# State-space stage of a hybrid backbone: pair decays by a minimum of two differences of running sums, initial state entered token-major

## Chip, core, metric

One core of a Trainium2 chip. The time is the device time of one launch in microseconds, as the median of three runs: 1575.97 us for the kernel before (1575.73 to 1576.37).

## What is computed

Two layers of a diffusion backbone run over 256 tokens: 128 context tokens (group 0) and 128 latent tokens (group 1), model width 1024. A layer is a half-step SwiGLU, a mixer with three branches (a bidirectional state-space scan, differential attention, pooling), and another half-step SwiGLU. The change touches only the scan. The scan has 16 heads of width 64, a state of 64, four groups of B and C, and one chunk of 128 tokens, so that for one direction it is

```python
a = (dt * a_coef)                                  # (heads, 128 tokens), negative
a_cum = jnp.cumsum(a, axis=-1)
seg = a_cum[..., :, None] - a_cum[..., None, :]
decay_in = jnp.exp(jnp.where(causal, seg, -jnp.inf))
scores = einsum('bclhn,bcshn->bchls', ch, bh) * decay_in
y_diag = einsum('bchls,bcshp->bclhp', scores, xdt)
decay_from_start = jnp.exp(a_cum)
y_off = einsum('bclhn,bchpn,bchl->bclhp', ch, h_prev, decay_from_start)
```

The backward direction is the same on the reversed tokens; both are added. The initial state h_prev is zero for the context tokens and is an input for the latent ones, so y_off exists for group 1 alone.

## The kernel before

**The main stream.** Everything that multiplies by a weight runs as a list of tiles of 128x1024 weights in a fixed order (`plan`, L155). A weight tile is loaded (`raw`, L567 to 576), copied by ScalarE to a rounded high part (`wh`, `emit_hi` L578) and its remainder is formed by VectorE (`wl`, `emit_lo` L588). Every product is three matmuls, high by high, high by low, low by high (`mm3`, L629), into three rotating PSUM tiles `pm`. The high parts are made five tiles ahead of use and the low parts four (`HI_AHEAD`, `LO_AHEAD`), in `end` (L610).

**Side work.** All else, the scan too, is written as Python generators that are advanced between pairs of weight blocks of the main stream (`advance`, L534). A generator yields the engine that its next step begins on and what the step waits for; `Pace` (L335) keeps an estimated clock of each engine and of each buffer, and `due` (L528) lets a step on TensorE be issued when its inputs are estimated to be ready, and a step on another engine when that engine is estimated to be at most 4 us ahead of TensorE. Two generators of the list `gens` run at a time (`CONC`). So the order on each engine is fixed at build time; the waits are semaphores that the framework places. PSUM for side work is two tiles `s1` of one bank and one tile `s2` of two banks (L482 to 486). The names `s1` and `s2` stand in the trace as `s`. SBUF work tiles of 128x1024 come from one pool `big` of 27 (L50, L452). All loads are issued by SyncE in one queue.

**The mixer** (L1049) runs in this order: dt, the gate of the pooling branch, x/B/C; pooling input and Q in two halves; the pooling branch; K; V; then it waits, in the order of issue, for the scan to be issued (`settle` on "y"); z; the gates and projections of the scan branch, and of the attention branch after `flush` (all side work issued); the output. The scan's generators start as soon as x/B/C are there and run beside pooling input, Q, the pooling projection and K. The attention's scores start when K is there.

**The scan before.** `ssd_prep` (L1400) makes dt and a token-major, splits a into a rounded part `ah` and a rest `al`, and forms with two small matmuls the decay to the end of the chunk (`dd`). `ssd_core` (L1472) goes through four iterations: two halves of the heads (`hf`, eight heads each) by two groups (`g`). In each iteration and for each direction `rhs` (L1507) writes `rh` and `rl`, 128 tokens x 8 heads x 128: a triangle of ones times the value of a (one VectorE instruction for `ah`, eight ScalarE ones for `al`). A product with a constant triangle `cstr` sums over tokens and gives the pair differences: 2 directions x 2 banks x 2 parts = 8 matmuls of 512 columns into `s2`, one direction masked to zero where the other holds. One ScalarE exp of 128x1024 makes the decays `ex`; VectorE multiplies them by the masked scores `cbm`, once per direction (`E`); 16 matmuls with xdt give y in `py`. For g = 1, 8 more matmuls with the ones halves of `cstr` (L1580) put the running sums across partitions, exp and a product with C give `CE`, and 8 fp32 matmuls with the block-diagonal initial state `h04` (L1615) are added into `py` ahead of the others. The state is loaded once for each half (L1484). A plain fp32 matmul shows as two records in the trace; a rounded one (fp32r) and a transpose as one.

All compute instructions go through one helper, so the profile puts them on L397; loads are on L568.

Of the kernel before, what the change touches and what calls it, by code (L numbers as in the profile page):

```python
# [10 lines left out]
F32 = mybir.dt.float32  # L11
# [38 lines left out]
BIG_BUFS = 27  # L50
# [47 lines left out]
for _n, _w in (("ident", 128), ("ones", 128), ("sel", 2), ("uf", 128), ("ub", 128), ("p0", 128), ("p1", 128), ("p2", 128),  # L98
               ("p3", 128), ("cos", 128), ("sin", 128), ("perm", 128), ("mf", 128), ("mb", 128), ("oh0", 128),
               ("oh1", 128)):  # L100
    CST[_n] = (_o, _o + _w)
    _o += _w
CST_W = _o
CST_R0 = CST["mf"][0]
# [3 lines left out]
def constants():  # L108
# [12 lines left out]
    put("mf", k > m)  # L121
    put("mb", k < m)
    put("oh0", np.broadcast_to(m < 64, (P, P)))
    put("oh1", np.broadcast_to(m >= 64, (P, P)))
# [189 lines left out]
def pack_small(I):  # L314
# [8 lines left out]
    bd = np.zeros((DEPTH, P, 2, 8, P), np.float32)  # L323
    for T in range(8):
        for half in range(2):
            h = ho[2 * T + half]
            bd[:, 64 * half:64 * half + 64, :, T, 64 * half:64 * half + 64] = st[:, :, h].transpose(0, 3, 1, 2)
    return xT, cT, ck, cv, np.ascontiguousarray(bd.reshape(DEPTH, P, 2, 2, 4, P).transpose(0, 3, 1, 2, 4, 5)).reshape(DEPTH, 2, P, 1024)
# [99 lines left out]
def backbone(ctx: ExitStack, tc: tile.TileContext, seq, wst, wada, wa0, wrow, xT_d, cT_d, cB_d, ck_d, cv_d, h0_d, prm_d, cst_d,  # L428
# [59 lines left out]
    cst = cp.tile([P, CST_R0], F32, name="cst")  # L488
# [5 lines left out]
    cstr = cp.tile([P, 4, P], F32R, name="cstr")  # L494
# [485 lines left out]
    def setup_consts():  # L980
        load(cst[:, CST_E:], cst_d[:, CST_E:CST_R0])
        ld = tmp("t512", [P, 512])
        load(ld, cst_d[:, CST_R0:CST_W])
        yield "dve", ld
        V.tensor_copy(cstr.rearrange("p a b -> p (a b)"), ld)
# [414 lines left out]
    def ssd_prep(l, sd):  # L1400
# [44 lines left out]
        ah, al = t64("dtah", F32R), t64("dtal", F32)  # L1445
        yield "dve", a
        V.tensor_copy(ah, a)
        yield "dve", ah
# [7 lines left out]
        V.tensor_tensor(out=dd, in0=pd, in1=a[:, 0], op=ALU.subtract)  # L1456
        drop("s1", pd)
        yield "act", dd
# [11 lines left out]
        sd.update(dt=dt, ah=ah, al=al, dd=dd, Bn=Bn)  # L1470

    def ssd_core(l, sd, yv):  # L1472
# [8 lines left out]
        def prep(it):  # L1481
            hf, g = its[it]
            if g == 0:
                h0 = big()  # L1484
                load(h0, h0_d[l, hf])
                half_[hf] = [h0.rearrange("p (d t q) -> p d t q", d=2, t=4), None]
# [20 lines left out]
        def rhs(it, d):  # L1507
            hf, g = its[it]
            rh = v3(big(F32R), 8)
            rl = v3(big(F32R), 8)  # L1510
            uu = C("uf" if d == 0 else "ub")
            yield "dve",
            if d < RH_ACT:
                for h in range(8):
                    c = d * 16 + hf * 8 + h
                    S.activation(out=rh[:, h], in_=uu, func=AF.Copy, scale=sd["ah"].bitcast(F32)[:, g, c:c + 1])
            else:
                V.tensor_tensor(out=rh, in0=uu.unsqueeze(1).to_broadcast([P, 8, P]),
                                in1=sd["ah"][:, g, hd(hf)[d]].unsqueeze(2).to_broadcast([P, 8, P]), op=ALU.mult)
            yield "act",  # L1520
            for h in range(8):
                c = d * 16 + hf * 8 + h
                S.activation(out=rl[:, h], in_=uu, func=AF.Copy, scale=sd["al"][:, g, c:c + 1])
            state[it, d] = (rh, rl)

        yield from prep(0)
        yield from rhs(0, 0)
        for it, (hf, g) in enumerate(its):
            xdt, xw = state.pop(it)
            yield from rhs(it, 1)  # L1530
            if g == 0:
# [14 lines left out]
                half_[hf][1] = cbm  # L1546
# [16 lines left out]
            h04, cbm = half_[hf]  # L1563
            CE = []
            ps = None
            for d in range(2):
                rh, rl = state.pop((it, d))
                if d == 0:
                    yield "pe", rh, rl, "s2"
                    ps = ps2()  # L1570
                else:
                    yield "pe", rh, rl
                for q in range(2):
                    T_.matmul(ps[:, q, :], lhsT=cstr[:, d], rhs=rh[:, 4 * q:4 * q + 4], start=(d == 0), stop=False)
                    T_.matmul(ps[:, q, :], lhsT=cstr[:, d], rhs=rl[:, 4 * q:4 * q + 4], start=False, stop=(d == 1))
                if g == 1:
                    yield "pe", "s1"
                    pr = ps1(512)
                    rh4 = rh.rearrange("p (j h) t -> p j h t", h=2)
                    rl4 = rl.rearrange("p (j h) t -> p j h t", h=2)  # L1580
# [3 lines left out]
                    ce = tmp("ce", [P, 4, P])  # L1584
                    yield "act", pr
                    S.activation(out=ce.rearrange("p a b -> p (a b)"), in_=pr, func=AF.Exp)
                    drop("s1", pr)
                    CE.append(ce)
                rh = rl = None
            yield "act", ps  # L1590
            ex = big()
            S.activation(out=ex, in_=ps.rearrange("p a b -> p (a b)"), func=AF.Exp)
            drop("s2", ps)
            if it < 3:
                yield from prep(it + 1)
            for ce in CE:
                yield "dve", ce
                V.tensor_tensor(out=ce, in0=ce, in1=BC[:, 1, hf, P:].unsqueeze(1).to_broadcast([P, 4, P]), op=ALU.mult)
# [8 lines left out]
            if it < 3:  # L1607
                yield from rhs(it + 1, 0)
            yield "pe", E[0], E[1], "s1"
            py = ps1(512)  # L1610
            for j in range(4):
                sl = slice(j * P, (j + 1) * P)
                if g == 1:
                    for d in range(2):
                        T_.matmul(py[:, sl], lhsT=h04[:, d, j, :], rhs=CE[d][:, j], start=(d == 0), stop=False)  # L1615
                for d in range(2):
                    for half in range(2):
                        T_.matmul(py[64 * half:64 * half + 64, sl],
                                  lhsT=xdt[:, d, j * P + half * 64:j * P + half * 64 + 64],
                                  rhs=E[d][:, 2 * j + half], start=(g == 0 and d == 0), stop=(d == 1))  # L1620
# [191 lines left out]
```

## Time and profile before

| | |
|---|---|
| median of 3 runs | 1575.97 us |
| span of the profiled execution | 1579.0 us |
| TensorE matmul busy | 1547.9 us |
| VectorE busy | 1313.5 us |
| ScalarE busy | 877.7 us |
| GpSimd busy | 58.7 us |
| HBM read, written | 343.36 MB, 4.19 MB |

The profile is one execution. Its span, first to last instruction, is what the rows below add up to; it is 3.0 us above the median of the runs, and no time outside the span is shown. A matmul's own duration contains its way through the array, so matmuls overlap: the cost of one in a stream is read from the distance of starts, not from its duration. In the timeline, equal neighbours are merged into one row with a count.

### The profile page before, as it was taken

Reading aid. Unit: us, or ns where it says so; the run is one execution under the profiler, and the core shown is the slowest. Engines: PE = TensorE matmul, PEld = TensorE weight load, DVE = VectorE, ACT = ScalarE, POOL = GpSimd, SP = SyncE. Lnnn points to the kernel's source line nnn. Section 1 sums busy time; section 2 is a strip of 40 time slices with the busy share of each in tenths; the row PEclk is TensorE's granted clock in tenths of the full one; section 3 lists DMA queues with packets and bytes.
Section 4 is the critical chain, followed back from the end, with each engine's and each line's share of the span. In section 5 each row is a group of like instructions: output and inputs, shape, how many; then the busy total and the mean of one; then the engine's idle time right before and its main releaser. Section 6 shows DMA issues by size and latency. Waiting matters only on the chain.

```text
span 1579.0 us, 31076 instructions
## 1 busy us (share of the span) xinstructions
PE 1547.9 (98%) x12154; PEld 1449.6 (92%) x12154; DVE 1313.5 (83%) x2391; ACT 877.7 (56%) x1640; POOL 58.7 (4%) x65
## 2 busy tenths in 40 slices
PE   6999999999999999999999999999999999999997
PEld 4998889999979999899899998998998999999986
DVE  4777798988598997899989999898768889989754
ACT  3564447676467446644547544576746754665442
POOL 0000002000001100100001000100000010010000
PEclk9999999999999999999999999999999999999998
DMA  9698764553674666687765877555447457557652
GB/s 365 210 336 291 280 247 168 189 174 114 219 241 155 214 241 221 216 300 286 261 221 195 301 268 268 181 187 177 138 146 278 166 206 258 177 200 282 218 181 81
DMA packets 99171, 349.59 MB, mean 221 GB/s; under 512 B 10960, under 2 KB 14672, under 8 KB 98896
## 3 DMA queue, kind: packets, MB, share of 16 engines
q1 hardware_dynamic: 99024, 347.60, 62.4%
q8 instruction: 96, 1.57, 0.4%
q14 instruction: 51, 0.42, 0.1%
HBM read 343.36 MB, written 4.19 MB: 220 GB/s over the span
## 4 chain that ended last, share of the span: by engine, by line
PE 76%; issue 12%; DVE 7%; DMA 3%; ACT 1%; POOL 1%; DVEq 0%; SPq 0%; POOLq 0%; ACTq 0%
PE pm L397 67%; PE s L397 7%; DVE wl L397 2%; DVE big L397 2%; PE pa L397 2%; DMA big<-wada 2%; DVE t1k L397 1%; POOL osr L397 1%; DVE wide L397 0%; DMA t<-prm 0%; DMA x<-xT 0%; ACT big L397 0%; DVE sqa L397 0%; ACT L397 0%; ACT t1k L397 0%
## 5 line engine op out<-in xcount | busy, mean ns | idle before, releaser
L397 PE MATMUL pm<-big,wh 128*128 128x256 f32 (+2 forms) x6568 | 1288.8, 293 | 2.5 <-DVE wide L397 1.6
L397 PEld LDWEIGHTS pm<-big,wh 128*128 128x128 f32 x6568 | 1028.5, 189 | 46.3 <-issue 16.4
L397 PE MATMUL pm<-big,wl 128*128 128x256 f32 (+1 forms) x3592 | 1004.1, 281 | 0.0
L397 PEld LDWEIGHTS pm<-big,wl 128*128 128x128 f32 x3592 | 676.7, 188 | 2.4
L397 DVE TENSOR_TENSOR wl<-raw,wh 128x1024 fp32r<-128x1024 f32 x481 | 586.4, 1224 | 25.3 <-ACT wh L397 25.0
L397 ACT CAST wh<-raw 128x1024 fp32r<-128x1024 f32 x481 | 501.3, 1047 | 135.2 <-PE pm L397 105.4
L397 DVE SCALAR_TENSOR_TENSOR big<-big,big 128x1024 f32<-128x1024 f32 x198 | 241.4, 1219 | 9.7 <-DMA big<-wrow 8.6
L397 ACT CAST big<-t1k 128x256 fp32r<-128x256 f32 x88 | 35.8, 407 | 151.8 <-DVE t1k L397 151.8
L397 ACT ACTIVATE big<-x,amod 128x128 fp32r<-128x128 f32 x96 | 33.4, 396 | 100.9 <-DVE x L397 81.0
L397 PE MATMUL pm<-wh,big 128*128 128x512 f32 x256 | 88.5, 409 | 0.0
L397 DVE TENSOR_TENSOR wide<-pm,rb 128x258 f32<-128x258 f32 (+1 forms) x108 | 45.1, 421 | 39.2 <-PE pm L397 33.5
L397 DVE SCALAR_TENSOR_TENSOR x<-pm,mods,x 128x128 f32<-128x128 f32 x152 | 43.6, 343 | 37.1 <-PE pm L397 36.9
L397 ACT COPY big<-pm 128x256 f32<-128x256 f32 (+2 forms) x88 | 30.7, 372 | 59.2 <-PE pm L397 58.5
L397 PEld LDWEIGHTS pm<-wh,big 128*128 128x128 f32 x256 | 48.1, 188 | 13.2 <-issue 2.1
L397 DVE TENSOR_TENSOR big<-t1k,big 128x256 fp32r<-128x256 f32 x128 | 55.5, 438 | 1.6 <-ACT big L397 0.9
L397 ACT ACTIVATE t1k<-wide 128x128 f32<-128x128 f32 (+1 forms) x96 | 33.4, 395 | 38.3 <-DVE wide L397 38.2
L397 PE MATMUL s<-big,big 128*64 128x128 f32 (+4 forms) x528 | 51.4, 295 | 0.0
L397 PE MATMUL pm<-wl,big 128*128 128x512 f32 x128 | 50.4, 394 | 0.0
L397 ACT ACTIVATE t1k<-pm 128x256 f32<-128x256 f32 x58 | 22.3, 385 | 49.4 <-PE pm L397 49.4
L397 PEld LDWEIGHTS s<-big,big 128*64 128x64 f32 (+2 forms) x528 | 40.8, 163 | 5.9 <-issue 2.3
L397 DVE TENSOR_TENSOR big<-big,big 128x256 f32<-128x256 f32 (+1 forms) x64 | 39.9, 623 | 3.7 <-ACT big L397 2.3
L397 DVE SCALAR_TENSOR_TENSOR big<-big,cw,big 128x252 f32<-128x252 f32 (+1 forms) x96 | 39.2, 473 | 2.5 <-ACT big L397 2.5
(142 smaller groups left out, 1001.7 us busy)
## 6 DMA issues: line engine op xcount, KB each, us to landing
raw<-wst SPq DMA_DIRECT2D x486, 512.0 KB, 3.8
big<-wrow SPq DMA_DIRECT2D x96, 512.0 KB, 5.2
big<-wada SPq DMA_DIRECT2D x32, 512.0 KB, 5.8
big<-wa SPq DMA_DIRECT2D x16, 512.0 KB, 10.2
big<-cB SPq DMA_DIRECT2D x12, 512.0 KB, 7.0
big<-h SPq DMA_DIRECT2D x4, 512.0 KB, 4.7
x<-xT SPq DMA_DIRECT2D x1, 1024.0 KB, 6.0
ns<-t SPq DMA_DIRECT2D x8, 128.0 KB, 3.5
```

The source lines that it names most:

```text
L397: r = fn(*a, **k)
```

## The change

The pair decay of forward and backward is exp of the smaller of two differences: with running sums from both sides, the difference that belongs to the direction in force is negative and the other positive. So no triangles are written. `ssd_prep` forms both running sums by two matmuls of 64 columns, copies them token-major into `c4` (four copies, for four rows per head), transposes that (2 transposes), and keeps it rounded with its rest in rows (`ch`); 64 of these rows go into a stationary operand `ltc`, each half masked for a direction. `ssd_core` writes one moving operand for an iteration, `zc` (64 of its rows by VectorE from `ch`; the other 64 are constants), and forms the two differences in 2 matmuls for each half of 512 columns. ScalarE copies one to SBUF, VectorE takes the minimum with the other, ScalarE takes the exp: two rounds of this an iteration. The initial state is stored dense for both halves of heads in one tile, loaded once; for g = 1 two matmuls with 64 rows each give C times state token-major, VectorE multiplies by the decays `ec` and adds the directions to `ys`, and four transposing matmuls put `ys` into `py`. `big` has 25 tiles. The constants mf, mb, oh0, oh1 go, bm (16 columns) and ind (2) come.

```diff
-BIG_BUFS = 27
+BIG_BUFS = 25
...
+    put("bm", np.where(k < 64, 1.0, -1.0) * (k % 16 == m[:, :16]))
+    put("ind", k // 16 % 2 == m[:, :2])
...
-    cstr = cp.tile([P, 4, P], F32R, name="cstr")
+    ltc = cp.tile([P, 2, 2, P], F32R, name="ltc")
+    zc = [cp.tile([P, 8, P], F32R, name=f"zc{hf}") for hf in range(2)]
...
 def ssd_prep
-        ah, al = t64("dtah", F32R), t64("dtal", F32)
-        V.tensor_copy(ah, a)
-        V.tensor_tensor(out=al, in0=a, in1=ah, op=ALU.subtract)
-        pd = ps1(32)
-        T_.matmul(pd[:, 0:16], lhsT=C("ub"), rhs=a[:, 0, 0:16], start=True, stop=True)
-        T_.matmul(pd[:, 16:32], lhsT=C("uf"), rhs=a[:, 0, 16:32], start=True, stop=True)
+        pd = ps1(128)
+        for i, u in enumerate(("uf", "ub")):
+            T_.matmul(pd[:, 64 * i:64 * i + 64], lhsT=C(u), rhs=a.rearrange("p g c -> p (g c)"), start=True, stop=True)
...
+        for d in range(2):
+            V.tensor_copy(c4[:, :, :, d, :], p4[:, d, :, d, :].unsqueeze(2).to_broadcast([P, 2, 4, 16]))
+            V.tensor_tensor(out=dd[:, 16 * d:16 * d + 16], ..., op=ALU.subtract)
...
+            T_.transpose(pc[:, g * P:(g + 1) * P], c4[:, g].rearrange("p c d h -> p (c d h)"), C("ident"))
...
+        S.copy(ch.rearrange("p a b -> p (a b)"), pc)
...
+            S.activation(out=ec[:, :, :, d, :], in_=c4[:, 1, 0, d].rearrange(...), func=AF.Exp)
+        for q in (32, 96):
+            V.tensor_tensor(out=ch[q:q + 32], in0=v3(pc, 2)[q:q + 32], in1=ch[q:q + 32].bitcast(F32), op=ALU.subtract)
...
+            V.tensor_scalar(out=ltc[64:P, d], in0=ch[64:P].bitcast(F32), scalar1=C("ind")[64:P, d:d + 1], ...)
...
 def ssd_core
-            if g == 0:
+            if it == 0:
                 h0 = big()
-                load(h0, h0_d[l, hf])
+                load(h0, h0_d[l])
...
-        def rhs(it, d):
+        def lines(it):
+            V.tensor_tensor(out=zc[hf][0:64], in0=sd["ch"][0:64, g]..., in1=C("bm")[0:64, hf * 8:hf * 8 + 8]..., op=ALU.mult)
...
-                for q in range(2):
-                    T_.matmul(ps[:, q, :], lhsT=cstr[:, d], rhs=rh[:, 4 * q:4 * q + 4], start=(d == 0), stop=False)
-                    T_.matmul(ps[:, q, :], lhsT=cstr[:, d], rhs=rl[:, 4 * q:4 * q + 4], start=False, stop=(d == 1))
-                if g == 1:
-                    for half in range(2):
-                        T_.matmul(pr, lhsT=cstr[:, 2 + half], rhs=rh4[:, :, half, :], start=(half == 0), stop=False)
-                        T_.matmul(pr, lhsT=cstr[:, 2 + half], rhs=rl4[:, :, half, :], start=False, stop=(half == 1))
-                    S.activation(out=ce.rearrange("p a b -> p (a b)"), in_=pr, func=AF.Exp)
-            S.activation(out=ex, in_=ps.rearrange("p a b -> p (a b)"), func=AF.Exp)
+            for q in range(2):
+                yield "pe", ltc, zc[hf], "s2"
+                ps = ps2()
+                for d in range(2):
+                    T_.matmul(ps[:, d, :], lhsT=ltc[:, d, g], rhs=zc[hf][:, 4 * q:4 * q + 4], start=True, stop=True)
+                S.copy(eq, ps[:, 0, :])
+                V.tensor_tensor(out=eq, in0=ps[:, 1, :], in1=eq, op=ALU.min)
+                drop("s2", ps)
+                S.activation(out=eq, in_=eq, func=AF.Exp)
+            if it < 3:
+                yield from lines(it + 1)
+            if g == 1:
+                yield "pe", half_["h0"], "s2"
+                for half in range(2):
+                    pr = slice(64 * half, 64 * half + 64)
+                    T_.matmul(ps[:, half, :], lhsT=BC[pr, 1, hf, P:], rhs=half_["h0"][pr, hf], start=True, stop=True)
+                V.tensor_tensor(out=v3(yo, 16), in0=ps..., in1=sd["ec"]..., op=ALU.mult)
+                V.tensor_tensor(out=ys.rearrange("p j h q -> p h j q"), in0=y5[:, :, 0], in1=y5[:, :, 1], op=ALU.add)
...
-                V.tensor_tensor(out=ce, in0=ce, in1=BC[:, 1, hf, P:].unsqueeze(1).to_broadcast([P, 4, P]), op=ALU.mult)
...
+            if g == 1:
+                for j in range(4):
+                    T_.matmul(py[:, j * P:(j + 1) * P], lhsT=ys[:, j].rearrange("p h q -> p (h q)"), rhs=C("ident"),
+                              is_transpose=True, start=(j == 0), stop=False, skip_group_check=True)
...
-                        T_.matmul(py[:, sl], lhsT=h04[:, d, j, :], rhs=CE[d][:, j], start=(d == 0), stop=False)
```

## Rows read from the trace of the kernel before

**Rows 1.** Page, parts 1 and 4: engines' busy time; the chain by engine.

```profile
PE 1547.9 (98%) x12154; PEld 1449.6 (92%) x12154; DVE 1313.5 (83%) x2391; ACT 877.7 (56%) x1640; POOL 58.7 (4%) x65
...
PE 76%; issue 12%; DVE 7%; DMA 3%; ACT 1%; POOL 1%; DVEq 0%; SPq 0%; POOLq 0%; ACTq 0%
```

**Rows 2.** Stretches of layer 0: us, busy of each engine (instructions), clock, DMA.

```profile
core 0: us, PE busy (x) PEld busy (x) DVE busy (x) ACT busy (x) POOL busy (x), PEclk, DMA share, GB/s
...
330.00:343.00 13.00, 13.00 (x103) 10.79 (x102) 11.03 (x19) 11.08 (x27) 0.00 (x0) 1.00 0.34 125
343.00:402.00 59.00, 59.00 (x506) 52.78 (x505) 44.72 (x64) 35.76 (x81) 0.00 (x0) 1.00 0.38 126
402.00:436.00 34.00, 34.00 (x291) 34.00 (x290) 20.78 (x28) 18.03 (x29) 0.00 (x0) 1.00 0.73 259
436.00:500.00 64.00, 63.99 (x432) 54.74 (x431) 58.81 (x116) 44.87 (x126) 0.00 (x0) 1.00 0.59 197
...
525.00:597.00 72.00, 72.00 (x614) 72.00 (x614) 67.00 (x115) 32.31 (x51) 1.44 (x2) 1.00 0.64 227
597.00:680.00 83.00, 79.34 (x666) 76.41 (x665) 69.84 (x146) 53.15 (x97) 6.63 (x9) 1.00 0.65 228
```

**Rows 3.** Timeline, TensorE, scan of layer 0: start, length, instruction, count.

```profile
342.96 2.03 PE L397 MATMUL s<-big,cstr 128*128 128x512 f32 x8
344.83 0.39 PE L397 MATMUL pm<-wh,big 128*128 128x512 f32 x1
345.06 0.39 PE L397 MATMUL pm<-wl,big 128*128 128x512 f32 x1
...
345.52 0.60 PE L397 MATMUL s<-cst,big 128*128 128x128 f32 x4
345.87 0.48 PE L397 MATMUL pm<-wh,big 128*128 128x512 f32 x1
346.19 0.39 PE L397 MATMUL pm<-wl,big 128*128 128x512 f32 x1
...
350.24 1.97 PE L397 MATMUL s<-big,big 128*64 128x128 f32 x32
352.14 0.71 PE L397 MATMUL s<-cst,big 128*128 128x128 f32 x4
352.61 1.17 PE L397 MATMUL s<-big,cstr 128*128 128x512 f32 x4
...
368.11 0.61 PE L397 MATMUL s<-ce,big 128*128 128x128 f32 x4
368.64 0.66 PE L397 MATMUL s<-big,big 128*64 128x128 f32 x8
...
372.92 0.71 PE L397 MATMUL s<-big 64*128 64x128 f32 x8
```

**Rows 4.** Timeline, TensorE, attention scores on 64 rows in two halves.

```profile
460.22 1.13 PE L397 MATMUL s<-big,big 64*128 64x256 f32 x8
461.29 0.50 PE L397 MATMUL pm<-wh,big 128*128 128x512 f32 x1
```

**Rows 5.** Groups by form: busy us, mean ns, idle before.

```profile
L397 DVE TENSOR_TENSOR wl<-raw,wh 128x1024 fp32r<-128x1024 f32 x481 | 586.4, 1224 | 25.3 <-ACT wh L397 25.0
...
L397 DVE TENSOR_TENSOR big<-cst,dtah 128x1024 fp32r<-128x1024 f32 x16 | 19.5, 1218 | 0.0
...
L397 DVE TENSOR_TENSOR big<-s,dt 128x512 f32<-128x512 f32 x16 | 10.3, 685 | 4.1 <-PE s L397 4.1
...
L397 ACT COPY big<-s 128x512 f32<-128x512 f32 x12 | 7.4, 613 | 0.0
...
L397 DVE TENSOR_TENSOR big<-s,big 128x256 fp32r<-128x256 f32 x16 | 6.7, 419 | 10.2 <-ACT big L397 10.1
...
L397 DVE TENSOR_TENSOR ce<-ce,big 128x512 f32<-128x512 f32 x8 | 5.3, 686 | 0.6 <-ACT ce L397 0.6
...
L397 ACT ACTIVATE ce<-s 128x512 f32<-128x512 f32 x8 | 4.8, 600 | 8.4 <-PE s L397 8.4
```

**Rows 6.** Timeline, ScalarE: the exp and eight scaled triangles.

```profile
345.03 1.02 ACT L397 ACTIVATE big<-s 128x1024 f32<-128x1024 f32 x1 [2.86 <-PE s L397]
...
346.88 2.45 ACT L397 ACTIVATE big<-cst,dtal 128x128 fp32r<-128x128 f32 x8
```

**Rows 7.** Waits of the load queue: total us, times, longest.

```profile
SPq L568 <- DVE wl L397: 805.8, 313, 11.6
SPq L568 <- DVE big L397: 350.1, 119, 6.8
```

**Rows 8.** Waits of all engines, the one for weight loads.

```profile
ACT wh L397 <- DMA raw<-wst: 8.5, 7, 2.2
```

More of the change, by code (lines that the diff above doesn't have):

```diff
@@ L103 @@
 CST_W = _o
-CST_R0 = CST["mf"][0]
 CST_E = CST["uf"][0]
@@ L486, in ps2 @@
         return grab("s2", pp.tile([P, 2, 512], F32, tag="s2", bufs=1, name=nm("s2")))
-    cst = cp.tile([P, CST_R0], F32, name="cst")
+    cst = cp.tile([P, CST_W], F32, name="cst")
     prm = [cp.tile([P, PRM_R], F32, name=f"prm{l}") for l in range(DEPTH)]
@@ L980, in setup_consts @@
     def setup_consts():
[L981 to L985, printed above, removed]
+        load(cst[:, CST_E:], cst_d[:, CST_E:CST_W])
+        yield "dve", cst[:, CST_E:]
+        for d in range(2):
+            V.tensor_scalar(out=ltc[0:64, d], in0=C("ones")[0:64].unsqueeze(1).to_broadcast([64, 2, P]),
+                            scalar1=C("ind")[0:64, d:d + 1], scalar2=None, op0=ALU.mult)
+        for hf in range(2):
+            yield "dve",
+            V.tensor_copy(zc[hf][64:P], C("bm")[64:P, hf * 8:hf * 8 + 8].unsqueeze(2).to_broadcast([64, 8, P]))
     def setup_layer(l):
@@ L1505, in prep @@
             state[it] = (xdt, xw)
-        def rhs(it, d):
+        def lines(it):
             hf, g = its[it]
[L1509 to L1524, printed above, removed]
+            yield "dve", sd["ch"]
+            V.tensor_tensor(out=zc[hf][0:64], in0=sd["ch"][0:64, g].bitcast(F32).unsqueeze(1).to_broadcast([64, 8, P]),
+                            in1=C("bm")[0:64, hf * 8:hf * 8 + 8].unsqueeze(2).to_broadcast([64, 8, P]), op=ALU.mult)
         yield from prep(0)
-        yield from rhs(0, 0)
+        yield from lines(0)
         for it, (hf, g) in enumerate(its):
             xdt, xw = state.pop(it)
-            yield from rhs(it, 1)
             if g == 0:
@@ new lines, in ssd_core @@
+            if it < 3:
+                yield from lines(it + 1)
+            if g == 1:
+                yield "pe", half_["h0"], "s2"
+                ps = ps2()
+                for half in range(2):
+                    pr = slice(64 * half, 64 * half + 64)
+                    T_.matmul(ps[:, half, :], lhsT=BC[pr, 1, hf, P:], rhs=half_["h0"][pr, hf], start=True, stop=True)
+                yield "dve", ps
+                yo = big()
+                V.tensor_tensor(out=v3(yo, 16), in0=ps.rearrange("p h (c q) -> p (h c) q", c=8),
+                                in1=sd["ec"][:, hf].rearrange("p h d j -> p (h d j)").unsqueeze(2).to_broadcast([P, 16, 64]),
+                                op=ALU.mult)
+                drop("s2", ps)
+                yield "dve", yo
+                ys = tmp("ys", [P, 4, 2, 64], bufs=1)
+                y5 = yo.rearrange("p (h d j q) -> p h d j q", h=2, d=2, j=4)
+                V.tensor_tensor(out=ys.rearrange("p j h q -> p h j q"), in0=y5[:, :, 0], in1=y5[:, :, 1], op=ALU.add)
+                yo = None
@@ L1619, in ssd_core @@
                                   lhsT=xdt[:, d, j * P + half * 64:j * P + half * 64 + 64],
-                                  rhs=E[d][:, 2 * j + half], start=(g == 0 and d == 0), stop=(d == 1))
+                                  rhs=E[d][:, 2 * j + half], start=(g == 0 and d == 0), stop=(d == 1),
+                                  skip_group_check=(g == 1))
             if yv[hf] is None:
```

73 lines of the change are left out of this document (31 added, 42 removed).

## Prediction, made before the changed kernel was run

> **What bounds the kernel.** I read the page first. TensorE is busy for 98% of the span and makes up 76% of the chain that ended last; VectorE is at 83% and ScalarE at 56% [rows 1]. Over the whole span such shares can hide a stage with another limit, so the second view is the table of stretches for layer 0 [rows 2]. The scan core runs from about 343 to 402 us. There TensorE is busy for all of 59.00 us, VectorE for 44.72 and ScalarE for 35.76, at a granted clock of 1.00 (2.4 GHz). The stretches after it, to 500 us and from 525 to 597, have no idle TensorE either; the first one with a hole is 597 to 680, with 3.7 us. So work taken off TensorE inside the scan should move everything behind it forward, as long as VectorE, with 58.81 of 64 us taken in the attention stretch, does not become late. The third view is TensorE's timeline [rows 3], since a matmul's own length overlaps its neighbours: I take distances of starts. Layer 1 repeats the pattern, and each term counts twice.
>
> **What leaves TensorE.** Before, a layer has 48 matmuls of 512 columns with the triangles: 8 in each of four iterations, and 8 more in the two with g = 1. Eight of them take from 342.96 to 344.83, 1.87 us, or 0.234 each [rows 3]. Afterwards 16 such matmuls are left (two directions, two halves of columns, four iterations), so 32 go: 7.5 us. The fp32 matmuls with the initial state stand between the products with xdt. Such a block without them runs from 350.24 to 352.14, 1.90 us; with them from 368.11 to 372.92, 4.81 us [rows 3]. Two blocks lose 2.91 each: 5.8 us. Together 13.3 us for a layer.
>
> **What comes to TensorE.** C times state: two fp32 matmuls of 64 rows and 512 columns for each g = 1 iteration, in all four records of 512. The attention scores have the same shape with 256 columns: eight records take from 460.22 to 461.29, 1.07 us [rows 4], the same number of columns, so 1.07 for an iteration and 2.1 for a layer. Eight records on 64 rows in that time means the two halves run side by side; if they do not here, it is twice that, the upper bound. Four transposes of `ys` an iteration: four transposes take 0.35 (345.52 to 345.87) and 0.47 (352.14 to 352.61) [rows 3]; I take 0.41, or 0.8 a layer. Two transposes of `c4`: 0.2. Two matmuls for running sums are already there and only get wider. Each new burst of fp32 work costs the main matmul behind it a later successor: 345.87 to 346.19 is 0.32 against 0.23 from 344.83 to 345.06 [rows 3], 0.09 for each of three or four bursts, 0.3 in all. Together 3.4 us. The split of the difference matmuls into bursts of two is put at nothing: after a burst of the triangles the main matmul goes on at 0.23 (344.83), there is no such step.
>
> **The sum.** 13.3 less 3.4 is 9.9 us a layer, 19.7 for both. On the profiled span of 1579.0 that is 1559.3; the span stands 3.0 above the median of the runs, so the forecast is 1556.3, rounded to **1556**. Its own range: C times state at twice the time makes it 4.3 longer, 1561. Below, TensorE might also lose its 3.7 us hole in 597 to 680 [rows 2] if the queues line up better, and the shorter transposes give 0.5: 1552, and 1551 taken as the end.
>
> **What is hidden.** VectorE loses eight 128x1024 triangles (1.22 each), four products with C (0.69) and three small ones, 13.1 us a layer. It gains four `lines` (no 64-row form is in the trace; as many columns, so 1.22), eight minima with one PSUM operand (0.685, the row of 128x512 from `s`), two products `yo` from PSUM (1.2), two sums `ys` (0.69), and some ten small ones at 0.2 to 0.42: 17.0 [rows 5]. That is 3.9 more. From 330 to 436 us VectorE is busy for 76.5 of 106 us [rows 2]; afterwards 80.4 of 96, or 84%, which TensorE covers. If the cover is gone, the whole 3.9 is paid, 8 us in both layers. ScalarE loses eight groups of eight triangles (2.45 each) and four exps of 1.02 [rows 6] and four of 0.60, 26.1 us; it gains eight copies (0.61), eight exps (0.60) and three small ones, 10.6 [rows 5]: a relief of 15 that nothing waits for, as TensorE is never idle there.
>
> **Waits and moves.** The new chain is, twice an iteration: TensorE, ScalarE copy, VectorE minimum, which frees `s2`, ScalarE exp. Behind the minimum on VectorE stand the low parts of weights (`wl`, 1.22 each, one for 24 matmuls); behind the exp on ScalarE the high parts and the copies out of `pm`. The low parts are made four tiles ahead of use, and a tile takes 24 x 0.117 = 2.8 us (291 starts in 34.00 us, [rows 2]), so a late minimum has 11 us before TensorE sees it in a weight; in `s2` it would see it at once. In `ssd_prep` one more trip, transposes, copy, rest, mask, delays the start of the core by perhaps 5 us; the scan must be issued before z, which comes after attention scores at 460 us [rows 4], and its last block ends before 402. One load of 512 KB a layer goes from the load queue, and the remaining one stays where the first was. `big` with 25 tiles gives up two, but the triangles held four and more at a time, so in the scan there is no lack; elsewhere loads may have to wait longer for a tile. The load queue already waits 119 times for VectorE to release a `big`, 6.8 us at the longest [rows 7], and ScalarE has lost only 8.5 us in all to weights not landed [rows 8].
>
> **A rule weighed against a row.** The trace puts 0.234 us on a 512-column matmul in a burst [rows 3]. The Trainium skill, "TensorE: Matmul & The Clock Gate", section "Back-to-back issue gap", gives about 131 ns for 512 columns in a stream of weight loads and matmuls; an estimate from that page is that 32 removed matmuls give back 4.2 us a layer and not 7.5, and the sum would end at about 1563. No row here shows such a distance, so the trace decides.
>
> **The rivals.**
>
> *Removed matmuls overlap more than their starts tell.* If each gave back only the distance of a main matmul, 0.117, the gain would be 7.5 us smaller in all: 1564. The page just named would lead to the same place. Against it: eight in a row keep their distance, and main matmuls start right behind them. Chance 0.03.
>
> *The tail of the scan falls into attention.* An iteration gets longer, as two round trips take the place of one and VectorE has 3.9 us more. If the last one slips behind 436 us, its VectorE work (two products of 1.22, a sum and two minima of 0.69, `yo` of 1.2 and about 1.1 of output, 8 us) meets a stretch in which 5.2 of 64 us are free [rows 2]; 3 to 4.6 us a layer fall to TensorE: **1565**. For it: the sequence of dependent steps; against: the 34 us from 402 to 436, with 13 free on VectorE [rows 2]. Chance 0.16.
>
> *Fewer tiles in `big` hold up the load queue.* Weights wait behind a load that waits for a tile. If a quarter of the 119 waits outgrow the reserve by 0.5 us each, 15 us are lost: **1571**. Against: the longest wait of 6.8 us now costs almost nothing [rows 7, 8]. Chance 0.10.
>
> *Slower: TensorE stands at `s2`.* The two-bank tile is single, and each of the 16 rounds (both layers) asks for it again after the minimum of the round before. If the estimate in `due` issues the next pair too early, TensorE waits in order. Break-even is 19.7 / 16 = 1.2 us a round; with one `wl` (1.22) queued ahead of the minimum (0.685) it is about 1.9, 30 us: **1586**. Against: in the scan before, under the same estimate, TensorE had no idle time [rows 2]. Chance 0.07.
>
> That the change does not do what it says, the two halves of C times state running one after the other, is inside the forecast's own range.
>
> **Chances.** Forecast 0.62, tail 0.16, load queue 0.10, `s2` 0.07, overlap 0.03, better than 1551 0.02. The range reaches from 1551 to 1570, the tail with some margin, and leaves out half of the load queue, `s2` and the better end, under 0.2. About 0.2%, 3 us, is what a measurement of this kernel can tell from no change. The load-queue case lies around that bound on the faster side; I give half of it to each. Faster 0.62 + 0.16 + 0.03 + 0.02 + 0.05 = 0.88, same 0.05, slower 0.07.
>
> **What would show it.** Right: in the new profile 32 records with `zc` and `ltc` in both layers (16 each) at 0.23 to 0.24 us from start to start; blocks with xdt for g = 1 at about 2.3 us instead of 4.81; the stretch from dt to z about 10 us shorter in each layer, with TensorE still at 1.00 of it; VectorE's busy time about 8 us up, ScalarE's about 30 down. Wrong: idle time of TensorE with `s` as its releaser in the scan (`s2`), attention scores that start late after K (tail), more than 8.5 us of waits of `wh` for weight loads (load queue), or a pair of 64-row records that start 0.43 apart rather than together.

## The result, and the profile after

The changed kernel takes 1561.94 us (median of 4 runs, 1559.84 to 1565.11) against 1576.17 for the kernel before beside it: ratio 0.9906, interval 0.9889 to 0.9923. That is 14.2 us less, where 19.7 were forecast: inside the range, 6 us above the forecast itself.

The page after, parts 1 and 4, for [rows 1]:

```profile
PE 1529.8 (98%) x12062; PEld 1435.4 (92%) x12062; DVE 1320.7 (85%) x2412; ACT 853.8 (55%) x1538; POOL 59.0 (4%) x65
...
PE 78%; issue 12%; DVE 6%; DMA 2%; ACT 1%; POOL 1%; DVEq 0%; POOLq 0%; SPq 0%
```

TensorE still bounds the kernel. VectorE has 7.2 us more (forecast about 8), ScalarE 23.9 less (forecast about 30). Of the missing 6, 5.1 us are four more loads of ScalarE's function tables (`ACT_TABLE_LOAD`, 17 where there were 13, 1.28 us each): in the last iteration of each scan an exp stands between two activations of another kind (411.39, 414.08 and 416.97 us in layer 0), with a load ahead of each. TensorE does not wait there. The span is 1559.7.

Stretches of layer 0 after, for [rows 2] (us, busy of each engine, granted clock, DMA):

```profile
328.00:341.00 13.00, 12.81 (x101) 10.55 (x101) 11.44 (x22) 7.18 (x15) 0.00 (x0) 1.00 0.34 123
341.00:400.00 59.00, 58.28 (x513) 54.92 (x512) 46.86 (x68) 28.34 (x45) 0.00 (x0) 1.00 0.46 152
400.00:425.90 25.90, 25.90 (x240) 24.19 (x239) 20.91 (x30) 17.02 (x28) 0.00 (x0) 1.00 0.74 256
425.90:490.00 64.10, 64.10 (x433) 54.78 (x431) 59.31 (x117) 45.40 (x126) 0.19 (x1) 1.00 0.60 198
```

Attention, the last row, now begins at 426 instead of 436. New are the hole of 0.72 us in the scan stretch and one of 0.19 in the stretch ahead of it: before, TensorE was busy for all of both.

TensorE's timeline after, scan of layer 0, for [rows 3, 4] (start, length, instruction, count):

```profile
341.41 0.64 PE L393 MATMUL s<-zc,ltc 128*128 128x512 f32 x2
341.89 0.40 PE L393 MATMUL pm<-wh,big 128*128 128x512 f32 x1
...
368.49 1.13 PE L393 MATMUL s<-big,big 64*128 64x512 f32 x4
369.54 0.50 PE L393 MATMUL pm<-big,wh 128*128 128x256 f32 x2
...
381.36 0.60 PE L393 MATMUL s<-cst,ys 128*128 128x128 f32 x4
381.89 1.97 PE L393 MATMUL s<-big,big 128*64 128x128 f32 x32
383.79 0.39 PE L393 MATMUL pm<-big,wh 128*128 128x256 f32 x1
```

Two difference matmuls take 0.48 us from start to start. C times state takes 1.05 (368.49 to 369.54), as the attention scores did; its four records start in two pairs, 7 ns apart within a pair, so the two halves run side by side. The four transposes take 0.53 and the block with xdt 1.90: 2.43 for g = 1, where it was 4.81.

The new operations by form (busy us, mean ns, idle before) have the prices that were taken for them, the 64-row `zc` with 1.21 too:

```profile
L393 PE MATMUL s<-zc,ltc 128*128 128x512 f32 x32 | 10.1, 396 | 0.0
L393 DVE TENSOR_TENSOR zc<-dtch,cst 64x1024 fp32r<-64x1024 f32 x8 | 9.7, 1209 | 0.0
L393 DVE TENSOR_TENSOR big<-s,dtec 128x1024 f32<-128x1024 f32 x4 | 4.9, 1217 | 1.7 <-PE s L393 1.7
```

**Where the time went.** I cut both traces at the same main matmuls (those into `pm`): the scan stretch runs from the start of the 1921st to that of the 2881st in layer 0, and from the 7281st to the 8257th in layer 1, attention included. Inside it every distance of starts is put down to one of these: side work (all that does not go into `pm`); entries (a main matmul next to side work, what it takes beyond 0.118 us, or 0.231 with 512 columns); gaps (any other main matmul that is over 0.04 late). The rest is main matmuls at their usual distance, 131.3 us in layer 0 of both kernels.

| stretch, us | total | side work | entries (count) | gaps |
|---|---|---|---|---|
| before, layer 0 | 179.88 | 44.37 | 3.96 (58) | 0.27 |
| after, layer 0 | 171.82 | 34.28 | 4.78 (76) | 1.43 |
| before, layer 1 | 180.06 | 44.32 | 3.96 (58) | 0.31 |
| after, layer 1 | 172.32 | 34.50 | 4.56 (74) | 1.41 |

Side work fell by 10.1 and 9.8 us. Entries give 0.8 and 0.6 of it back, gaps 1.2 and 1.1. The two scans gain 8.06 + 7.74 = 15.8 us.

Sorted by what stands next to the main matmul, the entries show where they come from. The 16 at a layer's difference matmuls (one ahead of and one behind each pair) come to 0.01 us together, and those at the triangles before to no more than 0.02. The rise is at plain fp32 work: main matmuls behind a block with xdt (0.10 each; four a layer, where it was one, since other side work followed the block directly), behind C times state (0.10 each, two a layer), and ahead of such bursts (0.09 each, two or three more a layer).

**The gap has one place.** TensorE's waits after, from 310 to 426 us (in total, times, longest); before, this view had none there:

```profile
PE pm L393 <- DVE big L393: 0.9, 2, 0.7
```

Both stand where the pooling branch multiplies its input by its map: the longer one in the map's second half, the other, of 0.19, at the same product of the first half (329.93). TensorE's timeline at the longer one:

```profile
364.46 0.28 PE L393 MATMUL pm<-big,wl 128*128 128x256 f32 x1
365.45 0.51 PE L393 MATMUL pm<-big,wh 128*128 128x256 f32 x2 [0.72 <-DVE big L393]
```

ScalarE's:

```profile
362.18 0.38 ACT L393 COPY big<-pm 128x256 f32<-128x256 f32 x1 [1.50 <-PE pm L393]
362.45 0.63 ACT L393 ACTIVATE big<-big 128x512 f32<-128x512 f32 x1
362.98 0.58 ACT L393 COPY big<-s 128x512 f32<-128x512 f32 x1
363.44 1.06 ACT L393 CAST wh<-raw 128x1024 fp32r<-128x1024 f32 x1
364.39 1.22 ACT L393 ACTIVATE big<-pm,prm 128x256 fp32r<-128x256 f32 x3
```

And VectorE's:

```profile
364.91 1.27 DVE L393 SCALAR_TENSOR_TENSOR big<-pm,prm,big 128x256 fp32r<-128x256 f32 x3 [2.37 <-ACT big L393]
```

This map needs little TensorE time for each product, and each product leaves its `pm` through ScalarE and then VectorE. The fourth has to wait until the first of three `pm` tiles is free. ScalarE comes to that evacuation at 364.39, because the exp (362.45) and the copy (362.98) of the pair decays stand in order ahead of it, with a weight's high part behind them. VectorE had idled 2.37 us for it. So the wait is not at `s2` but at `pm`, through ScalarE's order. In the kernel before, ScalarE was free at this place and waited for each product:

```profile
375.67 0.47 ACT L397 ACTIVATE big<-pm,prm 128x256 fp32r<-128x256 f32 x1 [3.70 <-PE pm L397]
376.39 0.47 ACT L397 ACTIVATE big<-pm,prm 128x256 fp32r<-128x256 f32 x1 [0.24 <-PE pm L397]
```

**Outside the scans.** The profiled spans differ by 19.3 us, near the 19.7 forecast, but by accident. The first main matmul starts 24.46 us into the span before and 21.16 after, and the stretch between the 3841st and the 4609th (feed-forward) takes 102.70 and 100.69: 5.3 us that I don't put down to the change, as these two vary from kernel to kernel whether they have it or not (20.8 to 23.3 and 99.8 to 102.1 in the others of this study); in the second, TensorE waits for loads of `wada`, 3.2 us before and 1.1 after. Against that the remaining stretches are 1.8 us longer after, but only 0.6 in the second profile of the changed kernel (*again*, below). Half of this difference lies ahead of the scan, where the granted clock was 0.91 from 21 to 41 us in the one and 1.00 in the other.

### The profile page after: what moved, and what is told of

Same layout as the page of the kernel before. It is cut to its first block, busy times and chain, and to the rows that moved or that the text cites. A ratio compares the mean times of both kernels' runs of the same rounds, so it can differ in the third digit from the quotient of the medians.

```text
span 1559.7 us, 30787 instructions
## 1 busy us (share of the span) xinstructions
PE 1529.8 (98%) x12062; PEld 1435.4 (92%) x12062; DVE 1320.7 (85%) x2412; ACT 853.8 (55%) x1538; POOL 59.0 (4%) x65
## 4 chain that ended last, share of the span: by engine, by line
PE 78%; issue 12%; DVE 6%; DMA 2%; ACT 1%; POOL 1%; DVEq 0%; POOLq 0%; SPq 0%
PE pm L393 70%; PE s L393 6%; DVE big L393 2%; DVE wl L393 2%; PE pa L393 2%; DVE t1k L393 1%; DMA big<-wada 1%; POOL osr L393 1%; ACT big L393 1%; ACT wh L393 0%; DVE wide L393 0%; DMA x<-xT 0%; DVE sqa L393 0%; ACT L393 0%; DVE x L393 0%
## 5 line engine op out<-in xcount | busy, mean ns | idle before, releaser
L393 PEld LDWEIGHTS pm<-big,wh 128*128 128x128 f32 x6568 | 1030.0, 189 | 52.7 <-issue 19.7
L393 PE MATMUL s<-big,big 128*64 128x128 f32 (+5 forms) x544 | 53.3, 303 | 0.0
## 6 DMA issues: line engine op xcount, KB each, us to landing
big<-wa SPq DMA_DIRECT2D x16, 512.0 KB, 10.1
```

Of the source, the lines that this page charges most:

```text
L393: r = fn(*a, **k)
```

## Experiments

Each was timed in five rounds beside the kernel before, whose medians were 1576.63 (runs of *again*, *state only*, *pairs twice*, *25 tiles*), 1576.32 (*less ahead*, *relu pair*, *lines twice*, *25 tiles and a gap*) and 1577.17 (the other four).

**Again.** The changed kernel, unaltered.

> The changed kernel unaltered, for a tighter ratio. Theory (TensorE work taken out of the scan, 10.1 us a layer, less 2.0 a layer given back as new burst entries and waits; nothing else changed): 15.5 to 16 us under the kernel before, ratio 0.990. If the 2.2 us that the two profiles differ by before the scan and the 1.7 us in the feed-forward part behind it belong to the change: 19 to 20 us, ratio 0.988.

1560.85 us, ratio 0.9900 (0.9886 to 0.9914). The scan stretches are 171.80 and 172.33 us, the same to 0.02. The gain is 14 to 16 us, as in the first of the two cases that were expected.

**The initial state alone** (before, with the token-major initial state; triangles and 27 tiles stay).

```diff
-                if g == 1:
-                    ... matmul(pr, lhsT=cstr[:, 2 + half], ...); exp; CE
+            if g == 1:
+                ps = ps2()
+                for half in range(2):
+                    T_.matmul(ps[:, half, :], lhsT=BC[pr, 1, hf, P:], rhs=half_["h0"][pr, hf], start=True, stop=True)
+                ... yo, ys; later four transposes into py
```

> Only the initial state is entered token-major; the triangles for the pair decays stay. Theory: a layer loses 16 matmuls of 512 columns at 0.234 (3.7) and the fp32 products in the blocks with xdt (5.8), and gains C times state (2.1), the transposes (1.1) and some entries (0.2 to 0.5): about 6 us a layer, 12 in all, so 1564 against 1576. Rival (a removed matmul gives back only the 0.117 of a main matmul): 3.7 less in all, 1568. Rival (it is the new pair decay that brings the gain): under 4 us, 1572 or more.

1572.70 us, ratio 0.9978 (0.9969 to 0.9987): 3.9 us gained, 8 short of the expectation and within the last rival, that the gain comes from the new pair decay. The trace speaks against that rival: the side work of layer 1 did fall by 6.15 us, as worked out; the scan stretch only by 3.2. TensorE's waits, 310 to 430 us:

```profile
PE pm L397 <- DVE big L397: 2.5, 1, 2.5
```

It is the same fourth product of the pooling map, and layer 1 has it too, with 2.5. Here VectorE's evacuation stood behind a low part, a triangle and another low part, one after the other without a pause, while ScalarE had evacuated in time (367.35):

```profile
366.05 1.22 DVE L397 TENSOR_TENSOR wl<-raw,wh 128x1024 fp32r<-128x1024 f32 x1
367.19 1.22 DVE L397 TENSOR_TENSOR big<-cst,dtah 128x1024 fp32r<-128x1024 f32 x1
368.32 1.22 DVE L397 TENSOR_TENSOR wl<-raw,wh 128x1024 fp32r<-128x1024 f32 x1
369.46 1.26 DVE L397 SCALAR_TENSOR_TENSOR big<-pm,prm,big 128x256 fp32r<-128x256 f32 x3
```

In layer 0 of this profile the granted clock also fell, after the wait:

```profile
360.00:380.00 20.00, 17.54 (x169) 16.34 (x168) 15.88 (x25) 10.92 (x27) 0.00 (x0) 0.91 0.34 119
...
1120.00:1140.00 20.00, 17.52 (x180) 16.30 (x178) 15.73 (x25) 13.43 (x34) 0.00 (x0) 1.00 0.29 101
```

The same hole in layer 1 is followed by no fall. In the profile the two waits (5.3 us more of gaps), the lower clock (1.6 of side work in layer 0) and the entries (0.8) make up 7.7 of the 8 us. How often the clock fell in the runs that were only timed is not on record, but their mean granted clock is: 0.997 in the profiled run and two others, which are the three fastest (1570.57 to 1571.84), and 0.994 to 0.996 in the other eight. So most runs lost more to the clock than the profile shows.

**The initial state alone, side work less ahead at the pooling map.** To test the wait as the cause, side work on ScalarE and VectorE is let only 0.5 us ahead of TensorE, not 4, from the last two Q tiles before each half of the map to the map's end.

```diff
+                if m >= 2:
+                    lag[0] = 0.5
...
+            lag[0] = LAG
```

> The kernel with only the token-major initial state, and around the pooling map the side work at most 0.5 us ahead instead of 4. In the trace of that kernel without this TensorE's work in the scan fell by 6.15 us a layer as worked out, but one wait of 2.5 us a layer came up, at the fourth product of the pooling map, for an evacuation behind scan work on ScalarE and VectorE. Theory (that wait, set by what is queued at this place, takes the gain): the wait goes, 4 to 5 us under the 1572.7 of that kernel, 1568. Rival (the wait only moves): 1572 to 1573.

1564.92 us, ratio 0.9925 (0.9910 to 0.9941): 7.8 us below the kernel without the two lines (0.9978 of before there), where 4 to 5 were expected, although no work was taken out. The wait is shorter, not gone:

```profile
PE pm L397 <- DVE big L397: 1.4, 1, 1.4
```

Between the two profiles the spans differ by 5.9 us, of which the scan stretches (178.33 and 176.83, then 175.32 and 174.40) hold 5.4. The gaps shrink by 1.3 and 1.1. Side work in layer 0 shrinks by 1.65, which is the lower clock, no longer there. So the place is shown. The four runs here have a mean granted clock of 0.998, where those without the two lines had 0.994 to 0.997: part of the 7.8 is the clock. That this hangs on the wait as well is likely, since the two lines touch nothing else, but not shown.

**Less ahead, with the change.** The same two lines in the changed kernel.

> The changed kernel, but from the third Q tile of each half to the end of the pooling map the side work on ScalarE and VectorE may be only 0.5 us ahead of TensorE by the estimate, where it was 4. Theory (TensorE waits 0.9 and 0.35 us a layer because the pooling map's evacuations stand behind scan work on ScalarE and VectorE): these waits go, 2 to 2.5 us under the changed kernel, 1558 to 1559. Rival (the waits only move to another place of the scan): no change, 1561. Rival (the scan gets so late that it pushes the attention): 1563 or more.

1560.96 us, ratio 0.9902 (0.9888 to 0.9915): no difference to the kernel without them, where 2 to 2.5 us less were expected; by its time it is the first rival. In its trace the wait is halved, and not moved to another place of the scan:

```profile
PE pm L393 <- DVE big L393: 0.4, 2, 0.2
```

The exp and the copy now stand behind the evacuations, and the wait in the second half of the map went from 0.72 to 0.19; the 0.19 in the first half stayed. The scan stretches are 0.6 us shorter each (171.26, 171.72), the stretch from the 4609th to the 7281st main matmul 0.6 longer. So the wait's cause is shown in the trace; what it costs in the changed kernel is too little for the timed runs to tell.

**Each difference matmul twice.**

```diff
-                    T_.matmul(ps[:, d, :], lhsT=ltc[:, d, g], ...)
+                    for _ in range(2):
+                        T_.matmul(ps[:, d, :], lhsT=ltc[:, d, g], ...)
```

> The changed kernel with each of the 16 difference matmuls of a layer issued twice into the same place. Theory (each costs its distance of 0.233 on the path): 7.5 us more than the changed kernel, 1569 to 1570. Rival (overlap, 0.117 each): 3.7 more, 1566. If TensorE were not the bound in the scan: no change, 1562.

1575.63 us, ratio 0.9992 (0.9984 to 1.0001): 14 us above the changed kernel, 7.5 expected. Four of them in a row:

```profile
342.63 1.09 PE L393 MATMUL s<-zc,ltc 128*128 128x512 f32 x4
343.56 0.40 PE L393 MATMUL pm<-wh,big 128*128 128x512 f32 x1
```

0.93 for four, 0.233 each: the price of the forecast, and no sign of overlap. Side work grew by 4.5 in layer 0, of which 16 x 0.233 = 3.7 are these. Gaps grew by 1.7 (3.09 against 1.43): the wait at the pooling map is 2.4 here. This time VectorE is late, whose evacuation starts at 371.64, behind seven instructions that follow each other without a pause from 366.37. The scan stretches, 178.36 and 178.57, explain 12.8 of the 14; the profiled run is the fastest of the eleven (1573.76). So the price of a matmul is confirmed, and work ahead of the map can cost more than its own length, because it changes what stands in front of the evacuations.

**25 tiles under the kernel before; with a gap; 26 tiles; 24 tiles with the change.** The second puts an unused buffer of two tiles' size behind the pool, so that all that lies behind it stays where it was with 27.

```diff
-BIG_BUFS = 27
+BIG_BUFS = 25
...
+    gap = gp.tile([P, 8 * (NT + 2)], F32, name="gap")
```

> The kernel before with 25 tiles in the pool of work tiles and nothing else altered. Theory: no effect, 1576 within 1.5 us. Rival (fewer tiles hold up the load queue): 3 to 15 us more. If fewer tiles were what moved the feed-forward part: 2 us less.

> The kernel before with 25 work tiles and an unused tile of the size of the two missing ones behind them, so that everything behind the pool lies where it lay with 27. The kernel with 25 took 4.4 us more, and its trace shows no new wait but main matmuls 2 ns further apart in some stretches. If the place in SBUF of what lies behind the pool does that: back to 1576 to 1577. If it is which of the work tiles are used: still 1580 to 1581.

> The kernel before with 26 work tiles. With 25 it took 4.4 us more, also with a gap that keeps the rest in place. If the cost grows with the number of tiles taken away: 1578 to 1579. If it hangs on which tiles meet in a matmul, by chance of the count: anywhere from 1574 to 1583, not in between by rule; the spacing of main matmuls should then account for it.

> The changed kernel with 24 work tiles instead of 25. If fewer tiles cost time by waits for loads: 2 us more or worse, with more waits of the high parts for weights. If it is which tiles meet: 1558 to 1566 by chance, with the main matmuls' spacing explaining it.

| kernel | tiles | median, us | ratio to before (interval) |
|---|---|---|---|
| before, fewer tiles | 25 | 1580.99 | 1.0029 (1.0018 to 1.0040) |
| the same with the gap | 25 | 1580.68 | 1.0028 (1.0018 to 1.0039) |
| before, fewer tiles | 26 | 1578.76 | 1.0013 (1.0004 to 1.0021) |
| after, fewer tiles | 24 | 1565.46 | 0.9921 (0.9906 to 0.9937) |

One tile taken from the kernel before costs 1.6 us, two cost 4.4; one more taken from the kernel after costs 3.5 to 4.6 by the medians (1561.94 or 1560.85 in other sets of runs), and 2.4 to 3.3 by the ratios, whose intervals still overlap. With 26 tiles it is the time expected if the cost grows with the number taken away. It isn't the place of the other buffers: with the gap the cost stays. And it doesn't show in the load queue either, whose waits with 25 tiles under the kernel before hardly differ from [rows 7]:

```profile
SPq L568 <- DVE wl L397: 803.7, 312, 11.6
SPq L568 <- DVE big L397: 360.2, 123, 6.7
```

The scan stretches with 25 (180.10, 180.49) are those of before, and no wait of TensorE is new. What differs is the distance of main matmuls in stretches that have nothing else. One stretch, 850 to 900 us, of the kernel before:

```profile
850.00:900.00 50.00, 50.00 (x425) 50.00 (x425) 45.49 (x75) 30.08 (x48) 0.00 (x0) 1.00 0.75 269
```

And with 25 tiles:

```profile
850.00:900.00 50.00, 50.00 (x419) 50.00 (x419) 44.85 (x76) 29.13 (x46) 0.00 (x0) 1.00 0.74 264
```

TensorE is busy all the time at the same clock and gets six matmuls less done. Cut at the same main matmuls there (836 from the 5409th on), the median distance is 120 ns and not 118, the mean 120.1 and not 118.4. Between the layers' scans (4609th to 7281st main matmul) the same work takes 1.8 us longer with 25 tiles, 1.5 with 26, and 1.1 with 24 against the changed kernel's 25. Why a matmul starts later when other tiles are in use was not found out; the single profiles differ by about a microsecond in this, so only the medians carry the size.

The changed kernel with 25 tiles hardly has this sign: from the 4609th to the 7281st it takes 361.27 us (361.23 in *again*), against 360.96 before and 362.81 for the kernel before with 25, and the mean of the 836 is 118.6 ns. The other variants of it with 25 tiles lie between 118.8 and 119.5. So the number of tiles alone does not set the distance.

**`zc` written twice**: 8 more instructions of 1.21 us on VectorE.

> The changed kernel with the moving operand of the differences written twice: 4 more VectorE instructions of 64x1024, 4.9 us a layer, on VectorE alone. Theory (VectorE's added work is covered): under 1.5 us more, 1562. Rival (the tail of the scan falls into the attention stretch, VectorE is the bound): up to 9.8 us more, 1566 to 1571.

1563.04 us, ratio 0.9914 (0.9900 to 0.9927). VectorE is busy for 1330.5 us, 9.8 more; the time rose by 1 to 2. TensorE covers most of it, as was forecast for the 8 us that the change adds. The trace has one new wait, of 0.6 us a layer: in the last iteration a pair of difference matmuls waits for `s2` (until 411.11 in layer 0). The minimum that frees it came late, but not for VectorE's added work: VectorE had waited 2.03 us for ScalarE's copy (409.76), which stood behind a table load, two activations and a high part. The order of issue shifted here too.

**Both directions on ScalarE, no minimum**: relu of the negated differences, then exp, each over both directions; the masked product sorts them out.

```diff
-                S.copy(eq, ps[:, 0, :])
-                V.tensor_tensor(out=eq, in0=ps[:, 1, :], in1=eq, op=ALU.min)
-                S.activation(out=eq, in_=eq, func=AF.Exp)
+                S.activation(out=eq, in_=ps.rearrange("p a b -> p (a b)"), func=AF.Relu, scale=-1.0)
+                S.activation(out=eq, in_=eq, func=AF.Exp, scale=-1.0)
```

> Another form of the pair decay without a VectorE step between two ScalarE steps: ScalarE takes relu of the negated differences and exp of the negated relu for both directions (1024 columns each), and VectorE multiplies per half of columns with both masks at once; no copy, no minimum. TensorE's work is the same. Theory (TensorE bounds the scan; VectorE has 5.5 us a layer less, ScalarE 7 more): within 2 us of the changed kernel, 1559 to 1562. Rival (the round trip over VectorE holds TensorE back): 4 us or more faster, 1557 or less.

1564.52 us, ratio 0.9929 (0.9917 to 0.9942), some 3 us above the changed kernel, outside what was expected and against the rival. VectorE has 9.4 us less work and ScalarE 7.0 more, but the wait at the pooling map is 1.6 at its longest, and the scan stretches are 173.43 and 173.69. It is not ScalarE's added work that is late there: ScalarE evacuates in time (from 364.99), and VectorE comes to it only at 366.97, behind seven instructions without a pause from 361.17. The order at this place changed with the rest.

**The change without the initial state**: C times state, the product with the decays, the sum of the directions and the four transposes are left out.

> The changed kernel without the initial state: C times state, its product with the decays, the sum and the four transposes are left out, so the latent tokens start from a zero state. Theory (they cost what the trace shows on TensorE: 2.1 and 1.1 us a layer and 0.2 to 0.3 of entries): 7 us less than the changed kernel, 1554. Rival (they partly stand in a place where TensorE waits anyway): under 5 us less, 1556 or more.

1559.29 us, ratio 0.9887 (0.9871 to 0.9902), some 2 us below the changed kernel; 1554 was expected, and the rival's 1556 or more came. Side work fell by 2.8 us in layer 0 and by 1.6 in layer 1. TensorE's waits in the whole execution have a row that the changed kernel does not have:

```profile
PE s L393 <- ACT big L393: 3.4, 2, 1.7
```

Once in each layer, at 432.26 in layer 0, a step of attention waits 1.7 us for ScalarE, which stood behind a high part, a load of its tables and softmax steps. So in layer 0 what was left out was on TensorE's path with its own length, and half of it came back as this wait in another stage (the stretch gained 1.4 us), since the order of issue shifted with it. In layer 1 nothing is left of the gain: there the granted clock fell after the wait (0.91 from 1170 to 1190 us), where the same wait in layer 0 is followed by none (1.00 from 420 to 440). The rival is right in its number, though not in its reason: TensorE did not wait where the work was taken out.

## Why the prediction was right, and where it was off

**What leaves and comes to TensorE: right.** The terms without entries were 13.3 - 3.1 = 10.2 us a layer; side work fell by 10.1 and 9.8. Each came out near its row: 0.233 to 0.24 for a difference matmul, 1.05 for C times state, 0.53 (not 0.41) for the transposes of `ys`, 1.90 for a block with xdt. The figure of the Trainium skill, "TensorE: Matmul & The Clock Gate", section "Back-to-back issue gap", about 131 ns for 512 columns in a stream of weight loads and matmuls, does not hold here: four took 0.93 us. The forecast that it would have given, 1563, lies close to the result all the same, so the total alone could not have told the two apart; the distances of starts do.

**"The split of the difference matmuls into bursts of two is put at nothing": right.** The 16 places a layer where they meet main matmuls cost 0.01 us together.

**"0.09 for each of three or four bursts, 0.3 in all": too low.** Entries rose by 0.8 and 0.6 us. The price of one is right (0.08 to 0.11 behind transposes and plain fp32 matmuls of the scan); the count was not. The forecast took only the new bursts, and only the main matmul behind them. The one ahead pays 0.09 too, and three more blocks with xdt a layer now have a main matmul behind them.

**"Waits and moves": the step that failed.** It followed the minimum and the exp to the weights, which have a reserve of 11 us, and to `s2`. It named the copies out of `pm` as standing behind the exp, and gave them no price. These have no reserve but three tiles, and where products are short, in the pooling map, two instructions of 1.2 us together on ScalarE reach TensorE as a gap of 0.9, where it was 0.3. All gaps of this kind come to 1.1 to 1.2 a layer more than before. The variants show the same product waiting for VectorE instead, as long as 2.5 us; the forecast looked at neither engine's evacuations there.

**Fewer tiles in `big`, put at nothing in the forecast: a price under the kernel before, open under the change.** "In the scan there is no lack" holds by the scan stretches (180.10 and 180.49 with 25 tiles). The rival of fewer tiles had the right resource for the kernel before and, as far as the traces show, the wrong mechanism. Its sign, over 8.5 us of `wh` waiting for loads, did come:

```profile
ACT wh L393 <- DMA raw<-wst: 15.1, 10, 3.3
```

But the kernel with the initial state alone and less ahead has 27 tiles, 16.9 us of this wait and a gain of 12 us; and no wait of TensorE names a high or low part of a weight. The sign was badly chosen. The cost, 1.6 to 2.8 us for a tile under the kernel before, shows in the distance of main matmuls. Under the change that sign is 0.3 us and not 1.8; the changed kernel with 27 tiles wasn't tried, so what its two tiles cost is not shown.

**"The span stands 3.0 above the median": true, but of this one execution.** In the profile after, the run's own time stands 1.8 us above the span (1561.46 and 1559.7). The profiled execution of before then took about 1580.8 (an estimate from that difference), at the upper end of its runs, and had 5.3 us more than the one after in the start and in the feed-forward. The forecast of 1556 doesn't depend on it, as it is the median less 19.7. But the span that was forecast, 1559.3, meets the measured 1559.7 by luck.

**The sum again.** 19.9 us of side work less 1.4 for entries and 2.3 for gaps, and 0.4 in the rest of layer 1, gives 15.8 in the scans; less 1.8 in the other stretches makes 14.0, less the 0.6 of *again* 15.2. The medians say 14.2 and 15.8. So of what the forecast lacks, the gaps are the largest term that is shown.

**The other rivals.** Overlap is excluded by the 0.93. The tail did not reach attention, but came near it: the scan's last matmul ends at 420.2 and attention starts at 426.70, where it was 401.5 and 437.0. Of a reserve of 35 us, 6.5 are left, and 2.2 with `zc` written twice (425.4 and 427.6): the scan ends 19 us later although TensorE has less to do in it. `s2` was never waited for in the scan, and with `zc` written twice it was. VectorE's added work was covered, as *`zc` written twice* shows from the other side.

## What to carry to other kernels

Cost a step moved onto an in-order engine not only by who reads its result, but by the shortest reserve among all that the engine also serves: here three PSUM tiles where products are short. Parts of a change do not add up when they share such a place: the initial state alone gained 3.9 us, the same with two lines about the order of issue 12. A pool size that "is not short of anything" can still have a price, and the price under one kernel need not be that under another, so measure it with the change too. And look at what a gain in one place does to the reserve of the next: here the scan's end moved from 35 us ahead of attention to 6.5.

## What was not expected of the hardware

The distance of back-to-back main matmuls moved from 118 to 120 ns (median of 836) between two kernels that differ only in the number of work tiles, at a granted clock of 1.00 and without a new wait in the trace; the place of other buffers made no difference (1580.99 and 1580.68 us). What sets it is open. A main matmul behind transposes or plain fp32 matmuls of the scan came 0.08 to 0.11 us late, one next to the difference matmuls, which have rounded operands, not at all (0.01 us for 16). A hole of 2.5 us at TensorE was followed by a lower granted clock in one layer (0.91 over 20 us) and by none in the other (1.00). The same holds of the holes of 1.7 us in the kernel without the initial state (0.91 and 1.00); neither of the two holes of 2.4 us in the kernel with each difference matmul twice was followed by a lower clock (1.00 and 1.00).
